# First expert unit's tokens taken by TensorE instead of a gather, empty slots skipped, two adaLN groups on VectorE

## The chip, the cores and the metric

The kernel runs on one core of a Trainium2 chip. The metric is device time in microseconds (us) of one launch. One execution was profiled; all rows of a trace come from that one.

## The reference, cut to what matters

Two layers work on 512 tokens (256 context, 256 latent) of width 1024. Each layer modulates a normed input with adaLN values (a matrix product of the condition vectors), runs three token mixers, and then a mixture of experts: each token goes to two of 16 experts, and each expert is a SwiGLU of width 512. The last layer needs the latent tokens alone.

```python
for l in range(DEPTH):
    mod = (silu_c @ w_ada[l] + b_ada[l])            # also for the context: mod_c
    sh1, sc1, gt1, sh2, sc2, gt2 = jnp.split(mod, N_MOD, axis=-1)
    h = rmsnorm(x, norm1[l]) * (1.0 + sc1) + sh1
    y, yc = token_mixers(h, hc, ...)
    x = x + gt1 * y
    h = rmsnorm(x, norm2[l]) * (1.0 + sc2) + sh2
    x = x + gt2 * hier_moe(h, ...)                  # layer 0: context and latent together

def hier_moe(h, ...):
    # top-1 group by softmax, top-2 experts inside it, weights in combine
    for e in range(N_EXPERTS):
        a = jax.nn.silu(t @ w1[e]) * (t @ w3[e])
        y = y + combine[:, e:e + 1] * (a @ w2[e])
```

## The kernel before, in words

`mixers(l, ...)` runs a layer's mixers, `moe(l, xd)` its experts. All weights come in tiles of 128 x 1024 floats (512 KB). `wsplit` (L171) loads one by SyncE's DMA queue into a ring (`raw`, four buffers, and `rawx`) and splits it into a high half on ScalarE (L72) and a low half on VectorE (L73). The halves go into a ring of `SPL = 4` pairs, or, two of every six by the counter `turns[1]`, into two pairs of the pool `ex_` ("wide"). `mm3` (L181 to L183) makes each product with three TensorE passes over these halves.

The adaLN values of 24 groups in each layer are made in two ways. `ada` (L214) multiplies a loaded tile on VectorE (L226, L228), piece by piece: `q_ada` queues the pieces of the groups in `MIX`, and `fill(RATE...)` takes some after each unit of mixer work; a `done` step adds over the partitions on TensorE (L234). `ada_pe` (L242) makes the groups in `BUB` on TensorE (L250) while the routing runs.

Between mixers and experts stands the routing. The normed and modulated token is `(x * scale) * r + shift`, with `r` the reciprocal norm of the token. `chunk` writes the scaled tokens, tokens on partitions, into `xs`; the shift rows lie in `brow`, and a copy of them is put into the DRAM tile `h2d` (L782). In `moe`, ScalarE multiplies `xs` by `r` (L868), and GpSimd's queue adds `xs` onto `h2d` with accumulating DMAs (L870). Meanwhile VectorE works out each token's two experts, TensorE counts ranks (L910, result in `rp`), `places` compares ranks with slot numbers (L945), and `slots` turns that into the token number of every slot (L953, L970, L971). Each unit `u` has 128 slots: one expert in layer 0 (16 units), two experts that share the slots in layer 1 (8 units). An empty slot holds token 0 with weight 0.

`gather(ix, xf)` (L1017) fetches the 128 token rows of a unit from `h2d` by an indirect DMA on GpSimd's queue (L1020) into the only buffer `g`, and makes the matrix `GT`, which puts results back to tokens. Its `turn_x` transposes `g` on TensorE (L1028) and splits it into the pair `X` (L1030, L1031). `hidden` makes one of the two input products of an expert: four weight tiles, 24 TensorE passes. The order at the start is written out:

```python
blk = [block(0)]                       # block(u) calls gather for unit u
blk[0][2]()                            # turn_x of unit 0
h1 = hidden(source(seq[0][2]), 0, blk[0][0])
blk.append(block(1))
blk[1][2]()                            # turn_x of unit 1
```

After that `hidden(source(e), 1, ...)` makes the second product of unit 0's expert. `overflow_table` (L1124), some 60 small VectorE operations, stands behind the second expert in the text. The scheduler orders each engine's instructions by their place in the text among those that its own model holds ready, and an engine then runs them strictly in that order. The pool `route` (`tmp`: `xs`, `brow`, `mov` and others) is closed before `ex_` is opened in its place, so the first writes into `ex_` (wide halves, `over` of L1132 and L1130) wait until the DMAs out of `xs` have ended.

Of the kernel before, what the change touches and what calls it, by code (L numbers as in the profile page):

```python
# [6 lines left out]
F32 = mybir.dt.float32  # L7
F32R = mybir.dt.float32r
# [3 lines left out]
AF = mybir.ActivationFunctionType  # L12
OP = mybir.AluOpType
# [4 lines left out]
P = 128  # L18
D = 1024
KD = D // P  # L20
S = 256
# [3 lines left out]
NE = 16  # L25
# [9 lines left out]
POP = (3, 3)  # L35
GTB = 5


RAW, SPL = 4, 4
RAWX = (6, 2)  # L40
# [7 lines left out]
DT = (1, 4)  # L48


BUB = (range(22, 24), range(21, 24))
TR = range(11, 12)
MIX = (range(8, 22), range(12, 21))
MIX01 = range(11)

RATE = ((0.5, 0.8, 0.9), (0.15, 0.3, 0.35))
LATE = (6, 4)

NOWSPLIT = ((), (0, 2), (), (0, 1, 2, 3))
# [17 lines left out]
def trunk(tc, io):  # L77
    nc = tc.nc
    es = []

    def pool(name, bufs=1, **kw):
        cm = tc.tile_pool(name=name, bufs=bufs, **kw)
        return cm, cm.__enter__()
# [12 lines left out]
    def st_ps(shape, dt=F32):  # L96
        return ps.tile(shape, dt, name="st", tag="st", bufs=2)

    def y_ps(shape, dt=F32):
        return ps.tile(shape, dt, name="yy", tag="yy", bufs=2)  # L100
# [12 lines left out]
    iotan = con[:, C_IO:C_IO + 2 * S]  # L113
# [3 lines left out]
    tokid = cst.tile([P, 4], F32, name="tokid")  # L117
# [30 lines left out]
    turns = [0, 0]  # L148
# [180 lines left out]
    mark = [None]  # L329
# [117 lines left out]
    def mixers(l, xsrc, x):  # L447
# [3 lines left out]
        nt = N // P  # L451
# [313 lines left out]
        for s in range(nst):  # L765
# [7 lines left out]
            for k2 in range(2):  # L773
# [3 lines left out]
                                        ident)  # L777
                nc.scalar.copy(brow[:, s, k2 * 512:k2 * 512 + 512], bp.rearrange("p a n -> p (a n)"))

        h2d = dram.tile([N, D], F32, name=f"h2d{l}")  # L780
        for t in range(nt):
            nc.scalar.dma_start(h2d[t * P:(t + 1) * P], brow[:, t * P // S])  # L782
# [34 lines left out]
        x["ada"] = [ada_pe(l, g) for g in BUB[l]]  # L817
        more.extend(spare)
        ahead.extend(early)
        x.update(rms=rms, lp=lp, lb=lb, xs=xs, h2d=h2d)  # L820
        close(cm_m)
        x["cmx"], x["gx"] = pool(f"gx{l}", side="right")
        return x
# [10 lines left out]
    def moe(l, xd):  # L834
# [82 lines left out]
            nc.vector.tensor_reduce(out, r, axis=AX.X, op=OP.add)  # L917

        for j in range(2):
            nc.vector.tensor_copy(tw[j][:, :, 0], tokid[:, :nt])  # L920
        rank = rp[:, :nt]
        num, pj = iota, rj
        if NM == 2:
# [13 lines left out]
        for j in range(2):  # L937
            of_choice(pj[j], j, pos if NM == 2 else rank)

        def places(pl, num, r):  # L940

            sl = [pl.tile([P, nt, P], F32R, name=f"sl{j}") for j in range(2)]
            for j in range(2):
                for t in range(nt):
                    nc.vector.tensor_scalar(sl[j][:, t], num, r[j][:, t:t + 1], None, op0=OP.is_equal)  # L945
            return sl

        def slots(sl, movs, n):
# [4 lines left out]
                nc.tensor.matmul(p_, sl[j][:, t], m(j, t), start=i == 0, stop=i == len(terms) - 1)  # L953
            return p_

        def main_slots(sl, i):

            return slots(sl, [lambda j, t, m=m: mov[j][:, t, i, m * NU:m * NU + NU] for m in range(NM)], NU)
# [8 lines left out]
        fill_mov(0)  # L967
        sl = places(tmp, num, pj)
        sp_ = main_slots(sl, 0)
        nc.vector.tensor_copy(idx, sp_)  # L970
        nc.vector.tensor_copy(slot[:, 0], sp_)  # L971


        ge = tt([P, nt, 4], "ge")
# [38 lines left out]
        close(xd["cmt"])  # L1013

        cm_n, ex_ = pool(f"exp{l}")

        def gather(ix, xf):  # L1017

            g = gx.tile([P, D], F32, name="g", tag="g", bufs=1)
            nc.gpsimd.indirect_dma_start(out=g, out_offset=None, in_=h2d,  # L1020
                                         in_offset=bass.IndirectOffsetOnAxis(ap=ix, axis=0))
            X = [gx.tile([P, KD, P], F32R, name=f"X{i}", tag=f"X{i}", bufs=2) for i in range(2)]

            def turn_x():
                for f2 in range(2):
                    p_ = st_ps([P, 4, P])
                    for f in range(4):
                        nc.tensor.transpose(p_[:, f], g[:, (4 * f2 + f) * P:(4 * f2 + f + 1) * P], ident)  # L1028
                    c = slice(4 * f2, 4 * f2 + 4)
                    nc.scalar.copy(X[0][:, c], p_)  # L1030
                    nc.vector.tensor_sub(X[1][:, c], p_, X[0][:, c].bitcast(F32))  # L1031

            GT = gx.tile([P, N], F32R, name="GT", tag="GT", bufs=GTB)

            nc.scalar.activation(GT, iotan[:, :N], AF.Abs, bias=xf, scale=-1.0)
            nc.scalar.activation(GT, GT.bitcast(F32), AF.Relu, bias=1.0, scale=-1.0)
            return X, GT, turn_x
# [11 lines left out]

        def gated(h1, h3, mine=None):  # L1050
            a = ex_.tile([P, FF], F32, name="a", tag="a", bufs=1)
            nc.scalar.activation(a, h1, AF.Silu)
            if mine is None:
                nc.vector.tensor_mul(a, a, h3)
            else:
                nc.vector.scalar_tensor_tensor(a, a, mine, h3, op0=OP.mult, op1=OP.mult)
            return a
# [136 lines left out]
            nc.vector.tensor_copy(ovs.rearrange("p b c -> p (b c)"), so)  # L1194

        def block(u):
            return gather(idx[:, u:u + 1], slot[:, 0, u:u + 1])

        def source(e):
            return lambda i: io["wmoe"][l, e, i]  # L1200
# [1 line left out]
        seq = [(u, m, e) for u in range(NU) for m, e in enumerate(members(l, u))]  # L1202
        if SPLX[l]:
            wide.extend((ex_, SPLX[l]))
        blk = [block(0)]
        blk[0][2]()
        sizes = list(GROUPS[l])
        group = []
        h1 = hidden(source(seq[0][2]), 0, blk[0][0])
# [2 lines left out]
        for i, (u, m, e) in enumerate(seq):  # L1212
            first, final = m == 0, m == NM - 1
            if final and u + 2 < NU:
                blk.append(block(u + 2))
            a = gated(h1, hidden(source(e), 1, blk[u][0]), own_[:, m, u:u + 1] if NM == 2 else None)
            if i + 1 < NE:
                h1 = hidden(source(seq[i + 1][2]), 0, blk[seq[i + 1][0]][0])
            aT = turn(a)
            if final and u + 2 < NU:  # L1220
                blk[u + 2][2]()
            if i == NE - 1:
                while between:
                    between.pop(0)()
            if first:
                yp_ = [mm_ps([P, 512]) for _ in range(2)]
            y = down(yp_, source(e), aT, wsl[:, u:u + 1], first, final, i == NE - 1)
            if final:
                group.append((y, blk[u][1]))
            if len(group) == sizes[0] and i < NE - 1:  # L1230
                between.extend(scatter(group))
                group = []
                sizes.pop(0)
            if i == 1:
                overflow_table()
        after = RmsP(xd["fin"], ex_, N)
        blocks = scatter(group, after)
        if not last:
# [17 lines left out]
        with tc.For_i(0, r) as it:  # L1256
            ev = nc.sync.value_load(tbl[:, bass.ds(it + 1, 1)], min_val=0, max_val=NE - 1)
            cur = ex_.tile([P, 3], F32, name="cur", tag="cur", bufs=1)
            nc.vector.tensor_copy(cur, ovs[:, bass.ds(it, 1)].rearrange("p a c -> p (a c)"))
            ci = ex_.tile([P, 1], I32, name="ci", tag="ci", bufs=1)  # L1260
            nc.vector.tensor_copy(ci, cur[:, 0:1])
            cw = ex_.tile([P, 1], F32, name="cw", tag="cw", bufs=1)
            nc.vector.tensor_add(cw, cur[:, 1:2], cur[:, 2:3])
            src = lambda i: io["wmoe"][l, bass.ds(ev, 1), i].rearrange("a p n -> p (a n)")
            X, GT, tx = gather(ci, cur[:, 0:1])
            tx()
            aT = turn(gated(hidden(src, 0, X), hidden(src, 1, X)))
            y = down([mm_ps([P, 512]) for _ in range(2)], src, aT, cw)
            for f_ in scatter([(y, GT)], after):
                f_()  # L1270
# [166 lines left out]
```

## Time and profile before

| | us |
|---|---|
| median of three runs | 1685.11 (1677.71 to 1685.37) |
| the profiled execution, its own time | 1678.52 |
| span of its instructions | 1676.7 |
| around the span | 1.8 |

The trace has 24504 instructions; TensorE is busy in 96% of the span, VectorE in 80%, ScalarE in 51%, and GpSimd in 4%. The four stages lie one behind the other: mixers of layer 0 up to 609 us, its experts from 639 to about 985 us, mixers of layer 1 from about 1002 to 1332 us, its experts from 1356 to 1664 us. A busy share says little by itself: what matters is which wait ends last in a stage, and the two stretches between mixers and experts are where TensorE stands idle.

### The profile page before, as it was taken

The numbers are of one execution on the slowest core, as the hardware profiler recorded it, in microseconds if no ns is written. First come the engines' busy times: TensorE is split into PE (matmuls) and PEld (weight loads), VectorE is DVE, ScalarE is ACT, GpSimd is POOL, SyncE is SP. The second block draws the span as 40 slices with busy tenths as digits, with TensorE's granted clock in tenths as the row PEclk, the third lists the DMA queues.
The fourth block names the chain that finished last, engine by engine and source line by source line (L and its number), as shares of the span: only waits on it lengthen the run. The fifth ranks groups of instructions, "written<-read, shape, count | busy, mean of one in ns | idle before, by whom it ended". The sixth has DMA issues, their size and how long they took to land. (4 is left out here: it accounts for less than half of the span.)

```text
span 1676.7 us, 24504 instructions
## 1 busy us (share of the span) xinstructions
PE 1617.6 (96%) x8909; PEld 1368.5 (82%) x8909; DVE 1343.8 (80%) x2421; ACT 860.6 (51%) x1131; POOL 59.2 (4%) x95
## 2 busy tenths in 40 slices
PE   7999999999999987999999999999999989999996
PEld 2888888888888866888888869999999868888885
DVE  6777779777675458999999958679887679999995
ACT  5523322222222347777778644334444567787873
POOL 0000000000000011000000010000000000000000
PEclk9999999999999998999999999999999989999998
DMA  8644336454454647999989734345776689999991
GB/s 315 195 126 126 120 117 197 164 166 161 140 174 138 251 130 269 345 321 315 320 314 335 268 104 137 122 142 170 267 249 226 204 267 361 358 351 353 342 329 46
DMA packets 104014, 378.71 MB, mean 226 GB/s; under 512 B 11464, under 2 KB 13768, under 8 KB 103632
## 3 DMA queue, kind: packets, MB, share of 16 engines
q1 hardware_dynamic: 95472, 348.74, 60.0%
q0 software_dynamic: 5216, 18.88, 3.8%
q10 hardware_dynamic: 3200, 9.46, 1.8%
q8 instruction: 72, 1.18, 0.3%
q14 instruction: 54, 0.44, 0.1%
HBM read 369.67 MB, written 11.56 MB: 227 GB/s over the span
## 5 line engine op out<-in xcount | busy, mean ns | idle before, releaser
L72 ACT CAST wh<-raw 128x1024 fp32r<-128x1024 f32 x319 | 332.4, 1051 | 444.5 <-PE mm L182 276.2
L73 DVE TENSOR_TENSOR wl<-raw,wh 128x1024 fp32r<-128x1024 f32 x319 | 385.3, 1219 | 56.9 <-ACT wh L72 51.9
L72 ACT CAST wh<-rawx 128x1024 fp32r<-128x1024 f32 x247 | 258.1, 1054 | 118.8 <-PE mm L183 78.4
L73 DVE TENSOR_TENSOR wl<-rawx,wh 128x1024 fp32r<-128x1024 f32 x247 | 294.3, 1219 | 19.4 <-ACT wh L72 15.7
L181 PE MATMUL mm<-hT,wh 128*128 128x512 f32 (+1 forms) x896 | 307.0, 343 | 0.1
L182 PE MATMUL mm<-hT,wh 128*128 128x512 f32 (+1 forms) x896 | 305.7, 342 | 0.0
L183 PE MATMUL mm<-hT,wl 128*128 128x512 f32 (+1 forms) x896 | 304.3, 340 | 0.0
L228 DVE SCALAR_TENSOR_TENSOR acc<-raw,sv,acc 128x256 f32<-128x256 f32 x476 | 203.0, 477 | 10.3 <-DMA raw<-in_wada_dram 10.3
L181 PE MATMUL mm<-wh,X 128*128 128x512 f32 x512 | 201.6, 394 | 0.7 <-issue 0.7
L182 PE MATMUL mm<-wl,X 128*128 128x512 f32 x512 | 201.4, 393 | 0.0
L183 PE MATMUL mm<-wh,X 128*128 128x512 f32 x512 | 200.3, 391 | 0.0
L183 PEld LDWEIGHTS mm<-hT,wl 128*128 128x128 f32 x896 | 169.6, 189 | 19.0 <-issue 0.5
L182 PEld LDWEIGHTS mm<-hT,wh 128*128 128x128 f32 x896 | 169.8, 190 | 18.7 <-issue 0.7
L181 PEld LDWEIGHTS mm<-hT,wh 128*128 128x128 f32 x896 | 169.8, 190 | 18.5 <-issue 0.5
L181 PEld LDWEIGHTS mm<-wh,X 128*128 128x128 f32 x512 | 97.0, 190 | 21.1 <-issue 1.3
L182 PEld LDWEIGHTS mm<-wl,X 128*128 128x128 f32 x512 | 97.0, 190 | 20.4 <-DVE wl L73 1.0
L183 PEld LDWEIGHTS mm<-wh,X 128*128 128x128 f32 x512 | 96.8, 189 | 20.0
L181 PE MATMUL mm<-wh,aTh 128*128 128x512 f32 x256 | 103.3, 404 | 5.1 <-ACT aTh L72 4.9
L182 PE MATMUL mm<-wl,aTh 128*128 128x512 f32 x256 | 100.2, 391 | 0.0
L1105 PE MATMUL yy<-GT,y 128*128 128x512 f32 (+1 forms) x384 | 95.1, 361 | 2.2 <-DVE xT L1109 2.1
L183 PE MATMUL mm<-wh,aTl 128*128 128x512 f32 x256 | 96.4, 397 | 0.0
L1105 PEld LDWEIGHTS yy<-GT,y 128*128 128x128 f32 x384 | 66.6, 188 | 14.3 <-issue 1.7
(344 smaller groups left out, 2588.2 us busy)
## 6 DMA issues: line engine op xcount, KB each, us to landing
rawx<-in_wmoe_dram SPq DMA_DIRECT2D x244, 512.0 KB, 5.2
raw<-in_wmix_dram SPq DMA_DIRECT2D x176, 512.0 KB, 4.0
raw<-in_wmoe_dram SPq DMA_DIRECT2D x140, 512.0 KB, 5.2
raw<-in_wada_dram SPq DMA_DIRECT2D x82, 512.0 KB, 3.8
rawx<-in_wada_dram SPq DMA_DIRECT2D x14, 512.0 KB, 10.2
dw<-dg ACTq DMA_DIRECT2D x8, 511.0 KB, 7.1
tab<-dw POOLq DMA_DIRECT2D x8, 384.0 KB, 4.7
h2d<-brow ACTq DMA_DIRECT2D x6, 512.0 KB, 6.5
```

The lines of the kernel that those rows point to most:

```text
L72: nc.scalar.copy(hi, src)
L73: nc.vector.tensor_sub(lo, src, hi.bitcast(F32))
L181: nc.tensor.matmul(out, st[0], mv[0], start=start, stop=False)
L182: nc.tensor.matmul(out, st[0], mv[1], start=False, stop=False)
L183: nc.tensor.matmul(out, st[1], mv[0], start=False, stop=stop)
L228: nc.vector.scalar_tensor_tensor(acc[v], w[:, k], s, acc[v], op0=OP.mult, op1=OP.add)
L1105: nc.tensor.matmul(p_, y[i][:, c], GT, start=gi == 0 and i == 0, stop=gi == ng - 1 and i == 1)
```

## The change

The first unit is no longer gathered. `oh` is a matrix of ones, tokens by slots, worked out from the rank of each token (`here`). TensorE multiplies `xs` by it, which selects and turns the tokens at once, and adds the shift row by one more product with `ind`, which says which stream a slot belongs to. Token numbers are kept plus one, so that 0 means an empty slot; `rows` turns 0 into an index beyond the table, and the indirect DMA skips it. `g` is one buffer, set to zero once. In layer 1 two groups of adaLN move from `BUB` (TensorE) to `MIX` (VectorE), and `RATE` rises. The split counter starts at 1, and `overflow_table` gets an order after the last SiLU.

```diff
-BUB = (range(22, 24), range(21, 24))
+BUB = (range(22, 24), range(23, 24))
-MIX = (range(8, 22), range(12, 21))
+MIX = (range(8, 22), range(12, 23))
-RATE = ((0.5, 0.8, 0.9), (0.15, 0.3, 0.35))
+RATE = ((0.5, 0.8, 0.9), (0.2, 0.4, 0.4))
...
+        shr = tmp.tile([64, D], F32, name="shr")
+        sel = tmp.tile([P, nst, 64], F32, name="sel")
+        nc.gpsimd.memset(shr, 0.0)
+        nc.gpsimd.memset(sel, 0.0)
+        for s in range(nst):
+            nc.gpsimd.memset(sel[:, s, 32 * s:32 * s + 1], 1.0)
+            nc.scalar.copy(shr[32 * s:32 * s + 1], brow[32 * s:32 * s + 1, s])
...
-            nc.vector.tensor_copy(tw[j][:, :, 0], tokid[:, :nt])
+            nc.vector.tensor_scalar(tw[j][:, :, 0], tokid[:, :nt], 1.0, None, op0=OP.add)
...
+        here = tmp.tile([P, nt, NM], F32, name="here")
+        if NM == 2:
+            nc.vector.tensor_tensor(here, pos[:, :, 0:NE:NU], mb[:, :, 0:NE:NU], op=OP.mult)
+            nc.vector.tensor_add(here[:, :, 0], here[:, :, 0], here[:, :, 1])
+        else:
+            nc.vector.scalar_tensor_tensor(here[:, :, 0], rank[:, :, 0], 1.0, mb[:, :, 0], op0=OP.add, op1=OP.mult)
+        oh = tmp.tile([P, nt, P], F32, name="oh")
+        for t in range(nt):
+            nc.vector.tensor_scalar(oh[:, t], iotan[:, 1:P + 1], here[:, t, 0:1], None, op0=OP.is_equal)
...
+        ip = y_ps([64, P])
+        for t in range(nt):
+            nc.tensor.matmul(ip, xd["sel"][:, t * P // S], oh[:, t], start=t == 0, stop=t == nt - 1)
+        ind = tmp.tile([64, P], F32, name="ind")
+        nc.scalar.copy(ind, ip)
+        for f2 in range(2):
+            p_ = st_ps([P, 4, P])
+            for f in range(4):
+                c = slice((4 * f2 + f) * P, (4 * f2 + f + 1) * P)
+                for t in range(nt):
+                    nc.tensor.matmul(p_[:, f], xd["xs"][:, t, c], oh[:, t], start=t == 0, stop=False)
+                nc.tensor.matmul(p_[:, f], xd["shr"][:, c], ind, start=False, stop=True)
+            c = slice(4 * f2, 4 * f2 + 4)
+            nc.scalar.copy(X_0[0][:, c], p_)
+            nc.vector.tensor_sub(X_0[1][:, c], p_, X_0[0][:, c].bitcast(F32))
...
+        def rows(ix, tok, s_, tmp_):
+            nc.vector.tensor_scalar(tmp_, s_, 0.0, SKIP, op0=OP.is_equal, op1=OP.mult)
+            nc.vector.tensor_scalar(tok, s_, -1.0, None, op0=OP.add)
+            nc.vector.tensor_tensor(ix, tok, tmp_, op=OP.add)
...
-        nc.vector.tensor_copy(idx, sp_)
-        nc.vector.tensor_copy(slot[:, 0], sp_)
+        rows(idx, slot[:, 0], sp_, none)
...
+        g = gx.tile([P, D], F32, name="g")
+        nc.vector.memset(g, 0.0)
...
+                nc.gpsimd.indirect_dma_start(out=g, out_offset=None, in_=h2d,
+                                             in_offset=bass.IndirectOffsetOnAxis(ap=ix, axis=0),
+                                             bounds_check=N - 1, oob_is_err=False)
...
+            return gather(idx[:, u:u + 1], slot[:, 0, u:u + 1], X_0 if u == 0 else None)
...
+        turns[1] = 1
         blk = [block(0)]
-        blk[0][2]()
...
-                overflow_table()
+                with tc.issue_after(mark[0].ins):
+                    overflow_table()
```

`mark[0]` is now the SiLU of `gated`, a ScalarE instruction; `issue_after` orders only those instructions of the block that run on the same engine.

## Rows read from the trace of the kernel before

**Rows 1.** The page, part 1: engine, busy us (share), instructions.
```profile
PE 1617.6 (96%) x8909; PEld 1368.5 (82%) x8909; DVE 1343.8 (80%) x2421; ACT 860.6 (51%) x1131; POOL 59.2 (4%) x95
```

**Rows 2.** Windows: start:end, length, busy us, clock, DMA share, GB/s; three long stages.
```profile
640.00:960.00 320.00, 319.85 (x1484) 262.74 (x1484) 307.75 (x400) 249.32 (x297) 16.56 (x15) 1.00 0.90 318
1366.00:1620.00 254.00, 249.89 (x1182) 206.52 (x1181) 236.41 (x267) 199.63 (x225) 5.80 (x6) 1.00 0.96 350
1005.00:1333.00 328.00, 325.98 (x2616) 318.91 (x2615) 259.92 (x534) 141.21 (x227) 6.33 (x19) 1.00 0.57 189
```

**Rows 3.** Windows of the stretch between mixers and experts, layer 0, then layer 1.
```profile
616.00:621.00 5.00, 5.00 (x37) 2.20 (x35) 4.01 (x26) 2.90 (x6) 1.69 (x2) 1.00 0.95 227
626.00:632.90 6.90, 0.45 (x3) 0.35 (x2) 0.17 (x1) 0.00 (x0) 0.00 (x0) 0.50 0.90 238
638.00:642.00 4.00, 4.00 (x14) 3.33 (x14) 2.29 (x9) 2.77 (x5) 0.98 (x1) 0.53 0.67 215
...
1340.00:1344.00 4.00, 4.00 (x24) 2.09 (x22) 2.83 (x28) 0.49 (x2) 0.00 (x0) 1.00 1.05 246
1352.00:1356.00 4.00, 1.09 (x4) 0.71 (x4) 0.00 (x0) 0.38 (x1) 0.00 (x0) 0.50 0.97 343
```

**Rows 4.** Timeline, layer 0: start, us, engine, line, operation, count, idle before with its releaser.
```profile
618.00 0.51 PE L910 MATMUL yy<-mb,tri 128*128 128x16 bf16 x14
619.08 1.65 DVE L945 TENSOR_SCALAR sl<-con,rj 128x128 fp32r<-128x128 f32 x8
623.84 2.61 PE L953 MATMUL yy<-mov,sl 128*128 128x16 f32 x15
632.90 0.24 DVE L1132 TENSOR_SCALAR over<-rj 128x4 f32<-128x4 f32 x2 [6.24 <-DMA h2d<-xs]
633.40 1.07 POOL L1020 DMA_INDIRECT g<-h2d,idx  x1 [15.43 <-DVE nq L1139]
637.81 1.94 PE L1028 MATMUL st<-con,g 128*128 128x128 f32 x8 [11.36 <-DMA g<-h2d,idx]
643.22 0.39 PE L181 MATMUL mm<-wh,X 128*128 128x512 f32 x1
643.91 0.39 PE L181 MATMUL mm<-wh,X 128*128 128x512 f32 x1
646.63 1.04 PE L1028 MATMUL st<-con,g 128*128 128x128 f32 x8
```

**Rows 5.** Timeline, layer 1, the same columns.
```profile
1339.21 0.28 PE L910 MATMUL yy<-mb,tri 128*128 128x16 bf16 x5 [0.84 <-DVE mb L905]
1341.06 0.87 DVE L945 TENSOR_SCALAR sl<-con,pj 128x128 fp32r<-128x128 f32 x4
1354.50 1.09 PE L1028 MATMUL st<-con,g 128*128 128x128 f32 x4 [3.68 <-DMA g<-h2d,idx]
1364.93 1.03 PE L1028 MATMUL st<-con,g 128*128 128x128 f32 x8
1365.72 0.48 PE L181 MATMUL mm<-wh,X 128*128 128x512 f32 x1
```

**Rows 6.** Prices: groups by line (busy, mean ns), and the same work in the timeline.
```profile
L792 PE MATMUL yy<-aw,xT 128*128 128x20 f32 x96 | 12.0, 253 | 0.0
599.38 0.96 PE L792 MATMUL yy<-aw,xT 128*128 128x20 f32 x8
1333.46 4.91 PE L250 MATMUL mm<-raw,sv 128*2 128x256 f32 x22
```

**Rows 7.** VectorE's adaLN work and its sum on TensorE; layer 1's fullest stretch, then L228 there.
```profile
L228 DVE SCALAR_TENSOR_TENSOR acc<-raw,sv,acc 128x256 f32<-128x256 f32 x476 | 203.0, 477 | 10.3 <-DMA raw<-in_wada_dram 10.3
546.62 0.94 PE L234 MATMUL st<-ones,acc 128*128 128x1 f32 x8
1140.00:1180.00 40.00, 39.53 (x325) 39.02 (x324) 36.87 (x90) 17.17 (x26) 1.39 (x9) 1.00 0.55 184
1140.00:1180.00 40.00, 9.32 (x21) 1.00 0.55 184
```

More of the change, by code (lines that the diff above doesn't have):

```diff
@@ L36 @@
 GTB = 5
+SKIP = 65536.0
 RAW, SPL = 4, 4
@@ L819, in mixers @@
         ahead.extend(early)
-        x.update(rms=rms, lp=lp, lb=lb, xs=xs, h2d=h2d)
+        x.update(rms=rms, lp=lp, lb=lb, xs=xs, h2d=h2d, shr=shr, sel=sel)
         close(cm_m)
@@ L938, in moe @@
             of_choice(pj[j], j, pos if NM == 2 else rank)
+        here = tmp.tile([P, nt, NM], F32, name="here")
[7 more added lines that the diff above has]
+            nc.vector.tensor_scalar(oh[:, t], iotan[:, 1:P + 1], here[:, t, 0:1], None, op0=OP.is_equal)
+        X_0 = [gx.tile([P, KD, P], F32R, name=f"X{i}", tag=f"X{i}", bufs=2) for i in range(2)]
+        ip = y_ps([64, P])
[13 more added lines that the diff above has]
+            nc.vector.tensor_sub(X_0[1][:, c], p_, X_0[0][:, c].bitcast(F32))
         def places(pl, num, r):
@@ L954, in slots @@
             return p_
+        def rows(ix, tok, s_, tmp_):
+            nc.vector.tensor_scalar(tmp_, s_, 0.0, SKIP, op0=OP.is_equal, op1=OP.mult)
+            nc.vector.tensor_scalar(tok, s_, -1.0, None, op0=OP.add)
+            nc.vector.tensor_tensor(ix, tok, tmp_, op=OP.add)
+        none = tmp.tile([P, NU], F32, name="none")
         def main_slots(sl, i):
@@ L1015, in moe, with gather @@
         cm_n, ex_ = pool(f"exp{l}")
[L1017 to L1022, printed above, removed]
+        g = gx.tile([P, D], F32, name="g")
+        nc.vector.memset(g, 0.0)
+        def gather(ix, xf, X=None):
+            if X is None:
+                X = [gx.tile([P, KD, P], F32R, name=f"X{i}", tag=f"X{i}", bufs=2) for i in range(2)]
+                nc.gpsimd.indirect_dma_start(out=g, out_offset=None, in_=h2d,
+                                             in_offset=bass.IndirectOffsetOnAxis(ap=ix, axis=0),
+                                             bounds_check=N - 1, oob_is_err=False)
             def turn_x():
@@ L1051, in gated @@
             a = ex_.tile([P, FF], F32, name="a", tag="a", bufs=1)
-            nc.scalar.activation(a, h1, AF.Silu)
+            mark[0] = nc.scalar.activation(a, h1, AF.Silu)
             if mine is None:
@@ L1196, in block @@
         def block(u):
-            return gather(idx[:, u:u + 1], slot[:, 0, u:u + 1])
+            return gather(idx[:, u:u + 1], slot[:, 0, u:u + 1], X_0 if u == 0 else None)
         def source(e):
@@ L1260, in moe @@
             ci = ex_.tile([P, 1], I32, name="ci", tag="ci", bufs=1)
-            nc.vector.tensor_copy(ci, cur[:, 0:1])
+            ct = ex_.tile([P, 2], F32, name="ct", tag="ct", bufs=1)
+            rows(ci, ct[:, 0:1], cur[:, 0:1], ct[:, 1:2])
             cw = ex_.tile([P, 1], F32, name="cw", tag="cw", bufs=1)
@@ L1264, in moe @@
             src = lambda i: io["wmoe"][l, bass.ds(ev, 1), i].rearrange("a p n -> p (a n)")
-            X, GT, tx = gather(ci, cur[:, 0:1])
+            X, GT, tx = gather(ci, ct[:, 0:1])
             tx()
```

## The prediction

> **What bounds the kernel now.** I read the page first: TensorE is busy in 96% of the span [rows 1]. The windows by stage then say where it counts. In the experts of layer 0 TensorE is busy in 319.85 of 320 us, in those of layer 1 in 249.89 of 254, in the mixers of layer 1 in 325.98 of 328 [rows 2]. So TensorE is the bound of each stage, VectorE is close behind it in the experts (307.75 of 320, 236.41 of 254), and time can be had only where TensorE stands: between mixers and experts. The windows there show 0.45 us of work in the 6.9 us up to 632.9 in layer 0 and 1.09 us in the 4 us up to 1356 in layer 1, both at a granted clock of 0.50, the 1.2 GHz level [rows 3]. The timeline names the chain of layer 0: the accumulating DMAs into `h2d` land at 632.9 (VectorE's `over` waits 6.24 us for them), the gather is issued at 633.4, and its rows are turned at 637.81, after 11.36 us of idle TensorE [rows 4]. In layer 1 the same last link is 3.68 us long and ends at 1354.5 [rows 5].
>
> **What the path is, measured at one point.** I compare both kernels where the second product of unit 0 is left to do. In layer 0 the second unit's turn starts at 646.63; by then 26 of the 48 passes of unit 0 are issued, so 22 are left behind it. Two first passes of `mm3`, three passes apart, start at 643.22 and 643.91: 0.23 us a pass, 5.5 for 24. The 22 end near 647.4 + 5.0 = 652.4 [rows 4]. In layer 1 the second product starts at 1365.72 with 24 passes left, end 1371.2 [rows 5].
>
> **Part 1, unit 0 on TensorE.** It removes the first gather's wait and one turn, and adds a computation. An f32 product is issued as two passes: the products of L792 number 8 chunks x 6 token tiles = 48, and the row has 96 records; eight of them, each with a 128x128 f32 stationary, take 0.96 us, 0.12 each [rows 6]. Those stream only 20 columns. The new ones stream 128; L250 streams 256 f32 columns in 4.91/22 = 0.22, so 128 take 0.11, which fits under 0.12 if load and stream overlap, and makes 0.23 if they don't. A turn is one pass with the same load and 128 columns, and eight take 1.03 us, 0.13 each, so they overlap; I take 0.12, and 0.23 as the other end. At the 1.2 GHz level eight turns took 1.94 us, 0.24 each [rows 4, 5].
>
> Layer 0 has 8 blocks x (4 + 1) + 4 = 44 products, 88 passes, 10.6 us. Their input `oh` follows the ranks: L910 ends at 618.5, four operations for the choices take 0.6 us (up to 619.1, where L945 starts), `here` 0.1 and four `oh` 4 x 1.65/8 = 0.8: 620.0 [rows 4]. The four products for `ind` run beside that, so the other 80 passes run from about 620.3 to 629.9, say 630.2 with the last of `ind`. TensorE is busy before (clock 1.00 from 616 on [rows 3]), so full clock. What was idle is now full, and what ran in the idle time counts: 8 slot products for the indices 0.9 us, 24 passes of the first product 5.5, 16 slot products 1.8 (0.11 each; 15 took 2.61 us in the stretch where the clock fell [rows 4]), the rest of L250 and its turns 1.4, the second unit's turn 1.0. That is 640.8, and 24 passes more end at 646.3. Gain 652.4 - 646.3 = 6.1 us.
>
> The second unit's gather is now the first. It waits for `h2d` (632.9) and for its indices, which stand behind the 88 passes: 630.2 + 0.9 and three small VectorE operations, 632. So it starts at 633.4 as the first one did, and lands at 637.8, two us before TensorE comes to it (639.8): hidden. If the skipped slots shorten it, nothing follows, since no later gather is waited for either; if the bounds test lengthens its issue (1.07 us now [rows 4]), up to 2 us are covered.
>
> Layer 1 has 8 x (2 + 1) + 2 = 26 products, 52 passes. `oh` is ready near 1341.8 (L945 starts at 1341.06; `here` and two `oh` come ahead of it, 0.7 us [rows 5]). Here the clock is open: before, 48 passes of adaLN filled TensorE and the clock was 1.00 in 1340 to 1344 [rows 3]; after, only 16 are left, 3.5 us from 1333.46 [rows 6], and TensorE stands from about 1337 to 1341.8. Between the ends of 52 x 0.12 = 6.2 us and 52 x 0.24 = 12.5 I take 18 passes at the lower level and 34 at the full one, 8.4 us: after the idle time of layer 0 the four us from 638 to 642 ran at 0.53, work without a gap [rows 3], and I take as much here. So 1350.2, then 0.9 + 5.5 + 1.8 + 0.3 + 1.0 = 9.5: the second product starts at 1359.7 instead of 1365.72. Gain 6.0 (8.2 at full clock, 1.9 all at the lower).
>
> The Trainium skill ("TensorE: Matmul & The Clock Gate", Part 1: The HAM clock gate) says that the array gets half its pulses when it has not been busy lately. By that rule layer 1's block is slower than by its count of passes, and removing adaLN work from the wait works against the block: 8.4 to 12.5 us by it, 6.2 without it. The 0.50 windows agree.
>
> **Part 2, adaLN groups of layer 1 to VectorE.** Removed from TensorE: 32 passes in a stretch where it waited, counted above. Added in the mixers: 2 x 16 operations x 0.477 = 15.3 us on VectorE, which has 260 of 328 us filled [rows 2, 7], four loads of 512 KB at a DMA share of 0.57, and 2 x 8 passes of L234 on TensorE, 2 x 0.94 = 1.9 us on the bound [rows 7]. Cover is thinnest where VectorE is busiest: 36.87 of 40 us in 1140 to 1180, with 9.32 us of L228 [rows 7]. The higher rate (0.4 for 0.3) adds a third, 3.1 us, and fills the window. I take 1 us of loss out of 0 to 4; with no cover at all it is 15.3.
>
> **Part 3, the rest.** The split counter puts the first four weight tiles into the ring, whose halves can be made early; before, the first one was wide and waited for `h2d` [rows 4]. The fifth now waits instead, but it is needed only after the first product. The order on `overflow_table` binds nothing, since its instructions run on VectorE and TensorE and the mark on ScalarE: `over` can still block VectorE until 632.9, and the low half of the second half of `X` behind it. That half is needed 12 passes, 2.7 us, after 631: covered, up to 1 us if not. Skipped rows save DMA traffic that is not the bound. Memsets and two row copies lie on GpSimd and ScalarE, 4% and 51% busy [rows 1]: nothing.
>
> **Sum.** 6.1 + 6.0 - 1.9 - 1.0 = 9.2 us less. The profiled execution would go from 1678.5 to 1669.3. It is 6.6 us under the median, 1685.1, at the low end of the runs; against the median the sum gives 1675.9, which I forecast as 1676.
>
> **Rivals.** *Slow f32 passes* (a load that doesn't overlap, or the lower clock throughout): 88 x 0.24 = 21.1 us ends layer 0's block 10.6 later than above, a loss of 4.5; layer 1 gains 1.9; with the 2.9 of part 2 that is 5.5 slower, 1691. It decides from 0.19 us a pass on, where 140 passes x 0.066 eat the 9.2. For it speaks that f32 streams twice as long per column; against it the turns at 0.13. *The queue order*: the second unit's turn may be put ahead of unit 0's first product, because the scheduler's model has the gather land sooner. TensorE then waits for 637.8 again, and near 1356 in layer 1: gain about 0.5 each, less 2.9, 1687. Against it: before, that turn stood behind the first product in both layers [rows 4, 5]. *VectorE takes over*: with 307.75 of 320 us it can't follow a TensorE that starts six us earlier with the overflow operations still to do; layer 0 keeps some 2 us, total 5, 1680. *The mixers of layer 1 bound by VectorE*: none of the 15.3 us is hidden; 6.1 + 6.0 - 1.9 - 15.3 = 5.1 slower, 1690. It decides once the added 3.1 us per 40 exceed what VectorE has free, which is 3.1 in the fullest window and more in the others.
>
> **How the numbers follow.** Forecast 0.63 (in four fifths of it over 0.5%, 8.4 us, about what a measurement can tell from no change), slow passes 0.10, queue order 0.09, VectorE in the experts 0.11, VectorE in the mixers 0.07. Low end: full clock in layer 1 and no loss in the mixers (12.4 less), and the runs at the low end of their spread (another 7 to 10): 1663. High end: the slower rivals, 1691. Faster by over 0.5%: 0.5; within: 0.38; slower: 0.12, since the slow rivals end near 0.3%.
>
> **What would show it.** Turns of unit 0 gone; 88 and 52 new f32 passes at 0.12; no idle of TensorE over 2 us between 620 and 650; the second unit's turn near 639.8 and 1358.7; in 1140 to 1180 PE still full. An 11 us wait before a turn, or passes at 0.24 in layer 0, would make it wrong.

## The result: 0.9% slower

The changed kernel takes 1694.59 us (median of 9 runs, 1691.50 to 1699.77), the kernel before 1678.18 beside it (9 runs, 1676.10 to 1685.37): a ratio of 1.0092, 95% interval 1.0073 to 1.0112. The profiled execution took 1694.87 us with a span of 1693.1. Lines move by 2 early in the file and by some 50 late: L72 is L74, L181 to L183 are L183 to L185, L250 is L252, L359 is L361, L910 is L920, L945 is L982, L953 is L990, L1028 is L1075. New are L963 (`ind`), L971 (tokens times `oh`) and L972 (the shift row, two passes of 64 rows each).

First the page, part 1 (engine, busy us, share, instructions), to set beside [rows 1]: TensorE is busy 24 us longer with 104 matmuls more, and the share rose to 97%. That share says nothing good: the waits were filled, and the span still grew.

```profile
PE 1641.3 (97%) x9013; PEld 1389.3 (82%) x9013; DVE 1357.0 (80%) x2466; ACT 862.6 (51%) x1134; POOL 63.7 (4%) x100
```

Then four stretches of the span, read from the timelines: A from layer 0's first L361 (the sum of squares ahead of its ranks) to the first L405 behind its experts; B the mixers of layer 1 up to their L361; C from there to the second unit's turn, when half of unit 0 is done; D the rest. What lies before A differs by up to 7.5 us between profiled executions of kernels that have nearly the same code there, so I compare A to D and take the medians for the whole.

| kernel | A | B | C | D | sum |
|---|---|---|---|---|---|
| before | 372.4 | 350.5 | 32.0 | 311.8 | 1066.6 |
| after | 374.4 | 354.6 | 39.7 | 312.8 | 1081.5 |

A itself is good to about 2 us only: behind L361 the granted clock is 0.50 for some 3 us in most profiles and for some 7 us in those of e6, e9 and e10, whose ranks come some 1.6 us later by it. Here is the window behind L361 in e5 and then in e9 (columns: start:end, length, busy us of PE, PEld, DVE, ACT, POOL, granted clock, DMA share, GB/s):

```profile
614.00:621.00 7.00, 7.00 (x28) 2.71 (x28) 5.09 (x26) 4.26 (x4) 4.46 (x4) 0.76 0.38 123
610.00:617.00 7.00, 7.00 (x22) 3.15 (x23) 4.20 (x26) 4.15 (x4) 3.42 (x4) 0.51 0.45 95
```

Half of the 14.9 us is C, the wait of layer 1. Its timeline on TensorE, to set beside [rows 5] (start, us, engine, line, operation, count, idle before with its releaser):

```profile
1341.15 3.62 PE L252 MATMUL mm<-raw,sv 128*2 128x256 f32 x16
1348.36 0.30 PE L920 MATMUL yy<-mb,tri 128*128 128x16 bf16 x5 [3.59 <-DVE mb L915]
1350.70 1.08 PE L963 MATMUL yy<-oh,sel 128*64 128x128 f32 x4 [2.04 <-DVE oh L959]
1351.71 1.22 PE L971 MATMUL st<-oh,xs 128*128 128x128 f32 x4
1352.87 0.79 PE L972 MATMUL st<-ind,shr 64*128 64x128 f32 x2
1353.59 1.22 PE L971 MATMUL st<-oh,xs 128*128 128x128 f32 x4
...
1366.70 3.57 PE L990 MATMUL yy<-mov,sl 128*128 128x8 f32 x16
...
1380.33 1.03 PE L1075 MATMUL st<-con,g 128*128 128x128 f32 x8
```

The gather's wait is gone, as meant. In its place the new block takes 16.0 us (1350.70 to 1366.70) for 52 passes, 1.88 for each chunk of four passes and a pair. Windows of the same place show the 1.2 GHz level all through it and into the first product, although TensorE is busy in 9.00 of 9 us. It is at full clock only from about 1377.8.

```profile
1358.00:1367.00 9.00, 9.00 (x31) 6.75 (x30) 0.69 (x1) 0.77 (x2) 0.00 (x0) 0.50 0.01 2
1372.00:1378.00 6.00, 6.00 (x18) 4.98 (x19) 4.72 (x27) 3.22 (x4) 1.07 (x1) 0.53 0.19 55
```

Layer 0, to set beside [rows 4]: the clock is full through the block, which takes 13.0 us (622.64 to 635.65). Eight L971 passes take 1.09 us, but each pair of L972 takes 0.41. The second unit's turn at 646.27 has 24 passes of unit 0 behind it, so unit 0 ends at 652.6. Before, it was 652.4.

```profile
622.64 1.06 PE L963 MATMUL yy<-oh,sel 128*64 128x128 f32 x8 [0.73 <-DVE oh L959]
623.63 1.16 PE L971 MATMUL st<-oh,xs 128*128 128x128 f32 x8
624.72 0.48 PE L972 MATMUL st<-ind,shr 64*128 64x128 f32 x2
625.13 1.16 PE L971 MATMUL st<-oh,xs 128*128 128x128 f32 x8
...
635.65 1.95 PE L990 MATMUL yy<-mov,sl 128*128 128x16 f32 x16
...
646.27 1.03 PE L1075 MATMUL st<-con,g 128*128 128x128 f32 x8
```

### The profile page after: what moved, and what is told of

It reads as the page before. It is cut to its first block, busy times and chain, and to the rows that moved or that the text cites. A ratio compares the mean times of both kernels' runs of the same rounds, so it can differ in the third digit from the quotient of the medians.

```text
span 1693.1 us, 24784 instructions
## 1 busy us (share of the span) xinstructions
PE 1641.3 (97%) x9013; PEld 1389.3 (82%) x9013; DVE 1357.0 (80%) x2466; ACT 862.6 (51%) x1134; POOL 63.7 (4%) x100
## 5 line engine op out<-in xcount | busy, mean ns | idle before, releaser
L74 ACT CAST wh<-raw 128x1024 fp32r<-128x1024 f32 x319 | 332.3, 1051 | 438.1 <-PE mm L184 247.0
L74 ACT CAST wh<-rawx 128x1024 fp32r<-128x1024 f32 x247 | 257.5, 1054 | 104.1 <-PE mm L185 72.9
L183 PE MATMUL mm<-hT,wh 128*128 128x512 f32 (+1 forms) x896 | 307.3, 344 | 2.2 <-ACT sig L724 1.5
L185 PE MATMUL mm<-hT,wl 128*128 128x512 f32 (+1 forms) x896 | 305.0, 341 | 0.8 <-DVE wl L75 0.8
L230 DVE SCALAR_TENSOR_TENSOR acc<-raw,sv,acc 128x256 f32<-128x256 f32 x504 | 215.6, 476 | 11.3 <-DMA raw<-in_wada_dram 11.3
L183 PE MATMUL mm<-wh,X 128*128 128x512 f32 x512 | 202.2, 395 | 0.0
L185 PE MATMUL mm<-wh,X 128*128 128x512 f32 x512 | 201.2, 393 | 0.0
L183 PEld LDWEIGHTS mm<-hT,wh 128*128 128x128 f32 x896 | 169.6, 190 | 20.8 <-ACT sig L724 1.7
L185 PEld LDWEIGHTS mm<-hT,wl 128*128 128x128 f32 x896 | 169.6, 189 | 20.5 <-DVE wl L75 1.2
L185 PEld LDWEIGHTS mm<-wh,X 128*128 128x128 f32 x512 | 97.1, 190 | 20.1
L183 PEld LDWEIGHTS mm<-wh,X 128*128 128x128 f32 x512 | 97.2, 190 | 19.6
L183 PE MATMUL mm<-wh,aTh 128*128 128x512 f32 x256 | 103.3, 404 | 7.1 <-ACT aTh L74 6.9
L185 PE MATMUL mm<-wh,aTl 128*128 128x512 f32 x256 | 96.6, 398 | 0.3 <-DVE aTl L75 0.3
L1152 PEld LDWEIGHTS yy<-GT,y 128*128 128x128 f32 x384 | 66.7, 188 | 14.5 <-issue 1.7
```

The costliest lines, as they stand in the source:

```text
L74: nc.scalar.copy(hi, src)
L183: nc.tensor.matmul(out, st[0], mv[0], start=start, stop=False)
L185: nc.tensor.matmul(out, st[1], mv[0], start=False, stop=stop)
L230: nc.vector.scalar_tensor_tensor(acc[v], w[:, k], s, acc[v], op0=OP.mult, op1=OP.add)
L1152: nc.tensor.matmul(p_, y[i][:, c], GT, start=gi == 0 and i == 0, stop=gi == ng - 1 and i == 1)
```

## The experiments

My theory when I set them up was that the clock is low in layer 1 because the adaLN products that filled the wait are gone, and that 64-row passes are a little dearer than assumed. The rivals put the loss on VectorE's added adaLN work, on the experts, or on the skip. Each kernel was timed beside the kernel before on the same chip.

| kernel | A | B | C | D | median us | ratio to before, 95% |
|---|---|---|---|---|---|---|
| e1 after, adaLN as before | 375.8 | 349.0 | 34.6 | 311.7 | 1685.79 | 1.0027 (1.0012 to 1.0042) |
| e2 before, adaLN moved | 372.4 | 354.8 | 29.6 | 311.5 | 1679.51 | 1.0002 (0.9987 to 1.0017) |
| e3 after, 128 rows | 371.1 | 354.8 | 28.8 | 313.2 | 1680.06 | 1.0003 (0.9986 to 1.0021) |
| e4 after, no skip | 374.9 | 354.8 | 36.8 | 312.8 | 1692.97 | 1.0074 (1.0051 to 1.0096) |
| e5 = e3 with e1 | 371.3 | 349.3 | 28.5 | 312.0 | 1673.56 | 0.9957 (0.9940 to 0.9974) |
| e6 before, counter | 374.4 | 349.3 | 31.7 | 311.7 | 1680.75 | 1.0001 (0.9984 to 1.0018) |
| e7 after, grouped | 373.7 | 355.9 | 31.1 | 312.7 | 1685.04 | 1.0020 (1.0002 to 1.0037) |
| e8 = e5, no counter | 371.8 | 349.3 | 31.3 | 310.3 | 1672.52 | 0.9942 (0.9920 to 0.9963) |
| e9 = e5, no skip | 370.4 | 348.9 | 28.5 | 311.8 | 1673.62 | 0.9970 (0.9956 to 0.9984) |
| e10 = e9, no counter | 372.0 | 350.0 | 29.3 | 313.8 | 1677.13 | 0.9989 (0.9975 to 1.0003) |
| e11 before, skip | 375.0 | 349.3 | 32.5 | 311.2 | 1679.72 | 1.0010 (0.9992 to 1.0027) |
| e12 = e5, layer 1 only | 374.3 | 349.6 | 28.5 | 311.7 | 1680.60 | 1.0007 (0.9992 to 1.0023) |

**e1, the adaLN groups back on TensorE.**

```diff
-BUB = (range(22, 24), range(23, 24))
+BUB = (range(22, 24), range(21, 24))
-MIX = (range(8, 22), range(12, 23))
+MIX = (range(8, 22), range(12, 21))
-RATE = ((0.5, 0.8, 0.9), (0.2, 0.4, 0.4))
+RATE = ((0.5, 0.8, 0.9), (0.15, 0.3, 0.35))
```

> The changed kernel with the adaLN groups of layer 1 put back on TensorE (BUB, MIX and RATE as before), all else as changed. Theory 1 (the clock): with 48 L250 passes in layer 1's wait the granted clock before the tokens' block is 1.00, its 52 passes end some 6 to 8 us after their start instead of 16, m0 starts at the full clock, and the mixers of layer 1 get back some 2 to 4.8 us: 1682 to 1686 in place of 1694.6. Rival 1 (the f32 passes are slow whatever the clock, the lower clock comes from their own kind of work): the block stays at .26 a pass and above, only the mixers' part comes back: 1690 to 1692. Rival 2 (the loss lies in the experts, by VectorE or the gather's skip): 1690 or more, with the layer 1 wait unchanged.

Measured: 1685.79 us. B falls by 5.6, C by 5.1. TensorE's timeline and a window of the block show full clock, and 9.0 us for the 52 passes instead of 16.0:

```profile
1340.51 7.46 PE L252 MATMUL mm<-raw,sv 128*2 128x256 f32 x26
1350.80 0.65 PE L963 MATMUL yy<-oh,sel 128*64 128x128 f32 x4
1351.38 0.71 PE L971 MATMUL st<-oh,xs 128*128 128x128 f32 x4
1352.02 0.49 PE L972 MATMUL st<-ind,shr 64*128 64x128 f32 x2
1352.43 0.71 PE L971 MATMUL st<-oh,xs 128*128 128x128 f32 x4
```
```profile
1351.00:1360.00 9.00, 9.00 (x54) 6.90 (x52) 2.20 (x17) 0.91 (x3) 0.00 (x0) 1.00 0.65 212
```

So the filler kept the clock up, and at full clock the changes of shape do not pull it down here. But even so the block is not the 52 x 0.12 = 6.2 us that the prediction has for a full clock: a pair still takes 0.41.

**e2, that part alone in the kernel before.**

```diff
-BUB = (range(22, 24), range(21, 24))
+BUB = (range(22, 24), range(23, 24))
-MIX = (range(8, 22), range(12, 21))
+MIX = (range(8, 22), range(12, 23))
-RATE = ((0.5, 0.8, 0.9), (0.15, 0.3, 0.35))
+RATE = ((0.5, 0.8, 0.9), (0.2, 0.4, 0.4))
```

> The kernel before with only the two adaLN groups of layer 1 moved to VectorE and the higher rate. Theory 1: the mixers of layer 1 lose 3 to 5 us (predicted at the start 2.9), and the wait of layer 1, where nothing but a gather goes on, gives back less than 1 us but its first product starts at the lower clock anyway: 1680 to 1683 against 1678.2. Rival (the mixers' 4.8 us of loss come from elsewhere, such as drift of the early stages): within 1 us of 1678.2.

Measured: 1679.51 us, no change. The mixers lose 4.3 us, as the theory had it, but the wait gives 2.4 back, which I had put under 1. So this part costs nothing where the wait is a gather's. The edit holds both the move and the higher rate; which of them costs the mixers was not tested.

**e3, the shift row over 128 partitions.** The added rows are zero.

```diff
-        shr = tmp.tile([64, D], F32, name="shr")
-        sel = tmp.tile([P, nst, 64], F32, name="sel")
+        shr = tmp.tile([P, D], F32, name="shr")
+        sel = tmp.tile([P, nst, P], F32, name="sel")
...
-        ip = y_ps([64, P])
+        ip = y_ps([P, P])
-        ind = tmp.tile([64, P], F32, name="ind")
+        ind = tmp.tile([P, P], F32, name="ind")
```

> The changed kernel with the product that adds the shift made over 128 partitions instead of 64 (shr and sel widened, the added rows zero), all else as changed. Theory: the 64-row weights are what makes these passes .2 us in place of .136 in layer 0 and .36 in place of .27 in layer 1; at 128 rows each of the 8 pairs falls from .41 to .27 there and from .72 to .54: 1.1 us and 1.4 us less, 1692 in all. Rival: the pair is slow because it ends an accumulation or waits for its input; times unchanged, 1694.6.

Measured: 1680.06 us, 14.5 less than the changed kernel, where I had expected 2.5. That the 64 rows make the loss was right, the size far off, for two reasons that the timelines show. In layer 0 not only the pair fell (0.41 to 0.23): the eight full passes ahead of it fell too, from 1.09 to 0.89. In layer 1 the clock now rises inside the block, at 1351.3, and the block takes 8.5 us (1345.61 to 1354.12).

```profile
621.62 1.06 PE L971 MATMUL st<-oh,xs 128*128 128x128 f32 x8
622.51 0.39 PE L972 MATMUL st<-ind,shr 128*128 128x128 f32 x2
622.74 1.06 PE L971 MATMUL st<-oh,xs 128*128 128x128 f32 x8
...
1346.60 1.06 PE L971 MATMUL st<-oh,xs 128*128 128x128 f32 x4
1347.45 0.63 PE L972 MATMUL st<-ind,shr 128*128 128x128 f32 x2
1347.88 1.06 PE L971 MATMUL st<-oh,xs 128*128 128x128 f32 x4
...
1351.29 0.39 PE L972 MATMUL st<-ind,shr 128*128 128x128 f32 x2
1351.52 0.61 PE L971 MATMUL st<-oh,xs 128*128 128x128 f32 x4
...
1354.12 1.93 PE L990 MATMUL yy<-mov,sl 128*128 128x8 f32 x16
```

That full passes slow down next to a 64-row pair says that the price lies in going from one shape to the other: a chunk took 1.50 us (623.63 to 625.13) and takes 1.12, so 0.19 each way at the full clock; in layer 1 at the lower one 1.88 against 1.28, 0.30 each way. The Trainium skill ("TensorEngine Tiling (Array Packing)", Tiling Modes) says that a change of the tiling mode drains the engine; the rows fit it and would give it a price here. That a drain is what takes the time no row shows.

**e7, the same 64-row passes in fewer stretches**, to tell the change of shape from the shape.

```diff
                 for t in range(nt):
-                    nc.tensor.matmul(p_[:, f], xd["xs"][:, t, c], oh[:, t], start=t == 0, stop=False)
-                nc.tensor.matmul(p_[:, f], xd["shr"][:, c], ind, start=False, stop=True)
+                    nc.tensor.matmul(p_[:, f], xd["xs"][:, t, c], oh[:, t], start=f == 0 and t == 0, stop=False,
+                                     skip_group_check=True)
+            for f in range(4):
+                c = slice((4 * f2 + f) * P, (4 * f2 + f + 1) * P)
+                nc.tensor.matmul(p_[:, f], xd["shr"][:, c], ind, start=False, stop=f == 3, skip_group_check=True)
```

> The changed kernel with the 64-row products of four chunks issued in a row behind the sixteen or eight full products, in place of one behind each chunk: the same passes, 2 stretches of 64 rows in a layer in place of 8. Theory A (each change between 64 and 128 rows costs TensorE about .2 us each way): the block of layer 0 goes from 13.0 to some 10.5 us, that of layer 1 at the lower clock from 16 to some 13, and if the stalls are also what keeps the clock down, it rises inside the block of layer 1: 1681 to 1687. Theory B (a 64-row pass is slow by itself and keeps the clock down by its rows): the block stays within .5 us of 13.0 and 16, 1694.

Measured: 1685.04 us, theory A. Eight 64-row passes in a row take 1.08 us, 0.135 each, hardly more than the others' 0.118; layer 0's block is 10.7 us (622.95 to 633.64). In layer 1 the clock rises within the block, near 1357, in the middle of the first stretch of 64 rows, and the block takes 9.2 us (1351.59 to 1360.81). So it was the 16 changes of shape, not the 64-row passes as such, with which the block of layer 1 ran at the lower level to its end; e4, which has them too, takes 15.4 us (1347.15 to 1362.52), at a granted clock of 0.50. In e1 and in layer 0 the same changes did not make a full clock fall inside the block; they go with a low clock that doesn't rise.

```profile
623.94 3.84 PE L971 MATMUL st<-oh,xs 128*128 128x128 f32 x32
627.71 1.16 PE L975 MATMUL st<-ind,shr 64*128 64x128 f32 x8
628.79 3.84 PE L971 MATMUL st<-oh,xs 128*128 128x128 f32 x32
...
1357.74 2.05 PE L971 MATMUL st<-oh,xs 128*128 128x128 f32 x16
1359.73 1.16 PE L975 MATMUL st<-ind,shr 64*128 64x128 f32 x8
```
```profile
1352.00:1358.00 6.00, 6.00 (x30) 5.32 (x29) 2.03 (x20) 0.41 (x2) 0.00 (x0) 0.58 0.54 106
1358.00:1361.00 3.00, 3.00 (x26) 2.76 (x25) 0.69 (x1) 0.52 (x2) 0.00 (x0) 1.00 0.02 5
```

**e4 and e11, the skip taken out, and the skip alone.** e4 undoes it in the changed kernel, e11 puts it into the kernel before:

```diff
             nc.gpsimd.indirect_dma_start(out=g, out_offset=None, in_=h2d,
-                                         in_offset=bass.IndirectOffsetOnAxis(ap=ix, axis=0),
-                                             bounds_check=N - 1, oob_is_err=False)
+                                         in_offset=bass.IndirectOffsetOnAxis(ap=ix, axis=0))
```

(With it go or come the offset of 1 in `tw`, `rows` and the cleared `g`.)

> The changed kernel with gathers that fetch all rows again: no bounds, no offset of 1 in the slots, and two buffers' worth of freedom as before (no cleared tile). Theory 1: the skip is off the path; within 1.5 us of 1694.6. Rival (the skip costs the experts: its longer index arithmetic, the clearing of g on VectorE or the added GpSimd work bring the 3.3 us that layer 0's experts lost): 1690 to 1692, experts of layer 0 back to 330 us.

> The kernel before with only the skip of empty slots in the gathers (bounds, the offset of 1, the cleared tile). Theory: GpSimd's power grows from 1.01 to 1.9 us and the ranks come 1.3 to 1.5 us later in each layer, the first gather with them, as far as it does not wait for its table in layer 0; a gather that moves less may land sooner and pay part of it back: 1679 to 1682 against 1679.9. Rival (the power is longer for the two memsets or the copies that the changed kernel puts on GpSimd and ScalarE, not for the bounds): power at 1.01 us, time unchanged.

Measured: 1692.97 and 1679.72 us. The experts were not touched by it, so that rival falls. But the skip is not off the path: in every kernel that has it GpSimd's power of the norm (the operation that makes `r`, on which the ranks wait) takes 1.85 to 1.92 us in layer 0, in those without it 1.01. e11 has neither the memsets nor the row copies and shows 1.85, so its rival falls too. GpSimd's timeline, after and then e4:

```profile
612.97 1.91 POOL L372 TENSOR_TENSOR rs<-ms,neghalf 128x4 f32<-128x4 f32 x1 [61.56 <-DVE ms L370]
```
```profile
610.21 1.01 POOL L372 TENSOR_TENSOR rs<-ms,neghalf 128x4 f32<-128x4 f32 x1 [61.67 <-DVE ms L370]
```

From L361 to the ranks it is 9.24 us after and 7.94 in e4 in layer 0, 7.74 and 6.21 in layer 1. The kernels without the skip whose clock is low for longer behind L361 (e6, e9, e10) show 9.56 to 9.57 in layer 0, so there the clock hides what the shorter power gives. In the time of the whole kernel that can't be told from nothing in e11. Why the power is longer was not found.

**e5, 128 rows and the old adaLN split together**, the edits of e3 and e1.

> The changed kernel with both: the shift product over 128 partitions, and the adaLN groups of layer 1 back on TensorE. Theory (the two costs are separate): the mixers of layer 1 return to about 350 us from 354.8, the wait of layer 1 from its first sum to the second unit's turn is some 31 us (34.6 with 64 rows and this adaLN split, less 3.2 for a block at .112 a pass; 28.8 with the adaLN groups moved): 1677 to 1678, the fastest so far. Rival (the adaLN groups cost the same wherever they stand): 1680 as with the 128 rows alone.

Measured: 1673.56 us, 0.43% under the kernel before (interval 0.26% to 0.60%) and some 1.3% under the change as it was made (0.9957 over 1.0092). The costs are separate, and C is even 2.5 us below what I added up, since the clock now stays full from the wait into the first product. The block of layer 1 takes 6.0 us, the 52 x 0.12 that the prediction has for a full clock:

```profile
1345.00:1351.00 6.00, 6.00 (x54) 5.90 (x54) 2.28 (x17) 0.85 (x2) 0.00 (x0) 1.00 1.00 322
1351.00:1357.00 6.00, 6.00 (x41) 4.05 (x41) 3.14 (x29) 3.48 (x8) 1.11 (x1) 1.00 0.32 102
```

**e6 and e8, the counter**, alone in the kernel before, and taken out of e5:

```diff
         turns[1] = 1
         blk = [block(0)]
```

> The kernel before with only the split counter set to 1 ahead of each layer's experts. Theory (VectorE's head start is what the experts lost): the counter alone changes nothing, experts of layer 0 as before (some 330 us), 1679. Rival (the counter puts other tiles into the ring and makes the 3.3 us): experts of layer 0 lose 2 to 3.5 us, 1681 to 1683.

> As the kernel with 128 rows and the old adaLN split, without the line that sets the split counter to 1. Theory (the counter is neutral): within 1 us of that kernel. Rival (the counter makes the loss in the experts): 2 to 3.5 us faster than it, experts of layer 0 some 330 us; or slower, if the wide first tile then stands in the way of the unit that no longer waits.

Measured: 1680.75 and 1672.52 us, no change that can be told in either. In e6 A is 2.1 longer, but 1.7 of it is there when the ranks come, by the clock behind L361. In e8 two effects cancel. Without the counter TensorE waits 2.1 us for the first high half, where e5 has no wait (in us: total, times, longest):

```profile
PE mm L183 <- ACT wh L74: 2.1, 1, 2.1
```

Unit 0 then ends 3.3 us later behind L361 than in e5 (41.2 and 37.9 us, to the end of its 48th pass; the low clock behind the block also lasts to 32.4 us there and to 29.0 in e5), but from there to the end of A it is 330.7 us in place of 333.4, and A is only 0.5 longer. So the counter is worth what the prediction's Part 3 says of it ahead of the experts, and its cost inside them was put at nothing. C is 2.8 longer and D 1.7 shorter, some 1.2 of both because the second unit's turn stands behind 29 passes of unit 0 there and not 24.

**e9 and e10, without skip, and then without counter.** Edits as above.

> The kernel with 128 rows and the old adaLN split, with gathers that fetch all rows as before. Theory (the skip is on the path ahead of the ranks): GpSimd's power of the norm falls from 1.92 to 1.01 us in layer 0 and from 1.61 to .69 in layer 1, and the ranks come 1.3 to 1.5 us sooner after the sum of squares in each layer (9.24 to 7.9, 7.93 to 6.3): 1671 to 1672 against 1673.6. Rival (what is saved there is lost in transfers, which fetch half as much again): no difference, 1673.6.

> As the kernel before it, and without the line that sets the split counter: of the change only the first unit's inputs by TensorE are left, with 128-row products. Theory: the gains add, 1670 to 1672. Rival (the counter and the skip hide one another's cost): 1673 or more.

Measured: 1673.62 and 1677.13 us; neither gained what I expected. The ranks of layer 1 do come sooner (7.07 instead of 7.93 us behind L361), but C of e9 stays at 28.5: with the adaLN products back, TensorE has no gap there that the ranks could shorten, and the products just stand behind the block instead of ahead of it. In layer 0 the ranks come 0.3 us later and not sooner, by the longer stretch of low clock. Why e10 is slower than e9 and e8 was not settled; 2 to 3 us of it are in D.

**e12, layer 1 alone**, layer 0's first unit gathered as before.

```diff
-        here = tmp.tile([P, nt, NM], F32, name="here")
+        X_0 = None
+        if NM == 2:
+            here = tmp.tile([P, nt, NM], F32, name="here")
...
         blk = [block(0)]
+        if X_0 is None:
+            blk[0][2]()
```

> The kernel with 128 rows and the old adaLN split, but layer 0's first unit is gathered and turned as before; only layer 1's is made by TensorE. Theory (layer 0's experts give most of its gain back, as VectorE and ScalarE can't follow): from the first sum of squares of layer 0 to the end of its experts 372 to 374.5 us in place of 371.3; 1674.5 to 1676.5 against 1673.6. Rival (the 5 us by which unit 0 ends sooner there are kept to the end): 1678 to 1679, no better than the kernel before by more than layer 1's 3.5.

Measured: A is 374.3, as the theory had it, but the time is 1680.60 us, nearer the rival's: the profiles of e5 and e12 are 3.0 us apart from A to D, the medians 7 (on two chips). Against e12, unit 0 of e5 ends 6.1 us sooner after L361 (37.9 and 44.0 us, to the end of its 48th pass), and the experts then take 3.1 us longer (333.4 and 330.3). By these two profiles about half of layer 0's gain is kept, by the medians all of it; that was not settled. Part of the 3.1 is seen as waits of TensorE (in us: total, times, longest), here in the changed kernel from 655 us to the end of the experts; before, only the last of these lines was there.

```profile
PE mm L183 <- ACT aTh L74: 1.7, 3, 0.8
PE mm L185 <- DVE aTl L75: 0.3, 1, 0.3
PE st L1075 <- DVE aTl L75: 0.3, 1, 0.3
PE yy L1152 <- DVE xT L1156: 1.3, 1, 1.3
```

## Why the prediction was wrong

**The step that failed** is the price of the block: all 88 and 52 passes at 0.12 us at the full clock (8.4 us for layer 1, with a part at the lower one), because the rows had no pass of this shape and I took the nearest, the 128x128 stationaries of [rows 6]. I named 0.23 as the other end for a load that doesn't overlap, and never asked what a stationary of 64 rows among those of 128 does. In layer 0 the 16 changes cost 16 x 0.19 = 3.0 us; in layer 1 they cost more by the clock, which with them stayed at the 1.2 GHz level for the 16.0 us of the block and 11 us behind it. Without them (e3) the blocks take 9.8 and 8.5 us, where the prediction has 10.6 and 8.4, split of the clock included. The rival *slow f32 passes* thus has the right place and, in layer 1, the lower clock throughout; its 0.24 a pass is too little there (16.0 / 52 = 0.31) and too much in layer 0 (13.0 / 88 = 0.15), since the changes of shape are in neither of its reasons. I had given it 0.10 and its 1691 is the nearest to the result.

The base was off too: the median of three runs that I forecast from, 1685.1, is 6.9 us above that of nine, 1678.2. From the latter the sum gives 1669.0, so 1676 lay nearer the result than the sum deserved.

The other terms, of which e3 gives the sum without that fault:

- **Layer 0 up to the end of unit 0.** Predicted 6.1 us sooner. With 128 rows it is 6.1 against a kernel that is otherwise the same (e5, e12); against the kernel before it is 4.7. The later ranks of the skip, 1.3 us, are the likeliest part of the difference; e9, without the skip, gains back 0.7, with the clock behind L361 against it. That `h2d` would no longer be waited for, and that the second unit's rows would land in time, was right: no wait for a gather is left.
- **Layer 0's experts.** I took the gain as kept. From the end of unit 0 to the end of A it takes 329.7 to 330.3 us in every kernel that gathers unit 0, 333.1 to 333.4 in the seven that have the block and the counter, and 330.7 and 331.3 in e8 and e10, with the block and without the counter. The size is that of the rival *VectorE takes over* (0.11), its reason only in half: e1 loses as much, and its unit 0 ends no sooner than before (42.55 and 42.58 us behind L361), so it is not a TensorE that starts six us earlier. What goes with the loss is its other half, the overflow operations still to do: behind the end of unit 0 VectorE has 382 operations and 313.2 us of work left before, 402 and 316.5 in e1, 387 and 313.0 in e8, and most of the added ones are the overflow table's. Windows from the end of unit 0 to the end of A, in the kernel before, e1 and e8:

```profile
652.69:982.51 329.82, 328.30 (x1521) 268.82 (x1520) 313.17 (x382) 251.39 (x299) 16.08 (x14) 1.00 0.87 305
657.67:990.92 333.25, 329.33 (x1521) 268.76 (x1519) 316.53 (x402) 255.86 (x305) 17.45 (x14) 1.00 0.84 294
654.26:984.90 330.64, 328.41 (x1520) 268.68 (x1519) 313.01 (x387) 252.65 (x302) 15.73 (x14) 1.00 0.85 294
```

  One cover is seen to go: before, seven of the eight slot products of the overflow table stood right behind the first turn of `a`, where TensorE now waits for `aTh`; in the changed kernel they come 27 us behind that turn. TensorE's waits account for some 2.4 of the 3.4 us. No run moves the overflow table alone, so that it is the cause is not shown.
- **Layer 1's wait.** Predicted 6.0 us of gain, measured 3.2 in e3 and 7.7 of loss in the change. In e3 1.5 of the difference is the later rank, again the skip that I had put off the path.
- **The mixers of layer 1.** Predicted 2.9 of loss, measured 5.5 (354.6 to 355.9 us, mostly 354.8, with the groups moved; 348.9 to 350.5, mostly 349.3, without). The passes of L236 were right: 16 more, 8.5 to 10.6 us. The 1.0 for VectorE's cover should have been some 3.4, within its 0 to 4. It isn't lost in 1140 to 1180, the fullest window of VectorE [rows 7], where TensorE has as much idle time as before, but 80 us later. Two rows of e3, a wait on ScalarE behind VectorE's work and the window in which TensorE lost most:

```profile
PE mm L183 <- ACT sig L724: 1.6, 1, 1.6
```
```profile
1220.00:1260.00 40.00, 38.08 (x316) 37.67 (x315) 32.57 (x64) 16.34 (x24) 0.00 (x0) 1.00 0.74 244
```

- **What was right**: the order of the queues (24 passes of unit 0 ahead of the second unit's turn in both layers) and what the counter does ahead of the experts (e8). The order on `overflow_table` was not tested alone; e12, which has it and gathers unit 0 in layer 0, has the slot products right behind the first turn of `a`, so that line by itself doesn't move them.

By these terms the forecast of 9.2 us of gain would have been, with the changes of shape left out as in e3, 4.7 - 3.4 + 3.2 - 4.3 - 1.4 (D) = a loss of 1.2 us, and the measurement of e3 is within 0.2% of no change. The sum failed on what was taken as covered as much as on the block.

## What to carry to other kernels

A product that fills a wait has to be priced with its own tile shape and with what it does to its neighbours: put passes of another row count together, or pad the rows with zeros, which here was worth 14.5 us of 1694.6. Work that keeps TensorE busy ahead of a block is worth its place, as it holds the clock; take it out of the wait only together with a look at what runs next. And time won ahead of a stage is not yet time won at its end: here the experts take 3.4 us longer in every kernel that has both the block and the counter, whether unit 0 ended sooner or not. Ask what the second engine, at 96% there, still has left to do when the stage begins.

## What the hardware showed that I had not expected

- TensorE at the lower level with no gap: 9.00 of 9 us busy at a granted clock of 0.50, for 16 us of the block. The Trainium skill ("TensorE: Matmul & The Clock Gate", Part 1: The HAM clock gate) has activity release the throttle; the busy time of the records alone did not, and e3 and e7 show the same count of passes doing so once the changes of shape are gone (e3) or fewer (e7). What the chip counts stays open.
- In layer 0 the clock also fell, to 0.57 in 640 to 644, after 13 us of the block, 24 slot products and the first passes of the first product, with TensorE busy in 4.00 of the 4 us. The changes of shape are not the reason: e3 shows the same (0.57 in 634 to 638). In e9 the clock stays at 1.00 there; why is open.

```profile
640.00:644.00 4.00, 4.00 (x12) 3.10 (x12) 3.79 (x36) 3.38 (x5) 0.05 (x1) 0.57 0.17 43
```

- A change between 64 and 128 rows of weights: 0.19 us each way at full clock, 0.30 at the lower level; a 64-row f32 pass of 128 columns in a row of its like, 0.135.
- GpSimd's power of a 128x4 tile: 1.01 us, and 1.85 to 1.92 in every kernel whose gathers test bounds.
